# The meta tokens' values from one stationary tile: u's high and low columns side by side

## The chip, the cores and the metric

The kernel runs on 1 core of one Trainium2 chip. The metric is the device time of one execution in microseconds (us); a lower time is better. Times before are 2316.95, 2318.2 and 2320.6 us, median 2318.2 us.

## The reference

One layer of a hybrid decoder: a Mamba-2 branch (SSD) and a gated-linear-attention branch (GLA), gated and merged. 16 learned meta tokens stand ahead of the 2048 real tokens; they feed the states of both branches and are dropped from the output. Cut to what the change touches:

```python
u = rmsnorm(hres, norm_w)                       # (16 + 2048, 1024)
z, xbc, dt_raw, q, k, v, g_gla, a_lr, merge_g = split_cols(u @ w_in, IN_WIDTHS)
...
# GLA, 4 heads, dk = 128, dv = 256; S_t = diag(a_t) S_{t-1} + k_t^T v_t
o_m, st_m = gla_chunked(q[:, :m], k[:, :m], v[:, :m], log_a[:, :m], N_META, st0)   # m = 16
o_r, _ = gla_chunked(q[:, m:], k[:, m:], v[:, m:], log_a[:, m:], GLA_CHUNK, st_m)
```

The state after the meta tokens is, per head, the sum over the 16 tokens of (k times its decay to the end) outer v: a matrix of 128 x 256. All arithmetic is float32.

## The kernel before

The first stage runs over the real tokens in 4 blocks of 512; block 0 has the 16 meta tokens as well (`m0` = 16). Each block does 4 SSD groups (`ssd_proj`) and then 4 GLA heads (`gla_proj`); the recurrences (`ssd_scan`, `gla_scan`) are generators that advance a step whenever a projection yields, so that their work stands between the projections'. The second stage (gates, branch projections, output) follows.

Matmuls of float32 precision are made of float32r passes: every operand is split into a high part and a low part, and `accum` makes three passes, high x high, high x low and low x high (lines 189 to 191). So the page shows each product as three lines. In `proj_tok` (values and z) 128 tokens of u are the stationary operand, 128 of its rows (one of 8 `kt`) at a time, and the weights' columns move. `u` is one tile with the high and low part, `whl` a tile of weights with both parts: in block 0 it is made from raw weights by ScalarE (ACT, line 176, the high part) and GpSimd (POOL, line 177, the low part), kept in DRAM, and loaded from there in later blocks. `proj_tok` loads two `whl` tiles, runs over all chunks of tokens, yields, and does the same with the other two.

For the values of a head in block 0 there are five chunks of tokens: four of real tokens and one that begins at token 0, whose first 16 rows are the meta tokens. All 128 rows of it are computed (PSUM tile `pv5`, in the trace `pt`), and the first 16 are copied to SBUF (`vm`, line 658; in the trace `c`). In `gla_scan`, `kd` (line 715, a tile `act`) is k times its decay. Its 16 meta columns are transposed by TensorE (PE, line 770), copied to SBUF (`btm`, line 772, a tile `bt`), and multiplied with `vm` to give the state `s_gla` (lines 784 and 785). The tiles with the tag `bt` share two buffers in turn; the SSD scan uses them too.

The order on PE and on SyncE (SP, which issues most DMAs) is that of the code, by hand; on VectorE (DVE), ACT and POOL the framework's scheduler chooses it.

Of the kernel before, what the change touches and what calls it, by code (L numbers as in the profile page):

```python
# [7 lines left out]
F32 = mybir.dt.float32  # L8
F32R = mybir.dt.float32r
BF16 = mybir.dt.bfloat16  # L10
U8 = mybir.dt.uint8
AF = mybir.ActivationFunctionType
ALU = mybir.AluOpType

P = 128
D = 1024
KT = 8
META = 16
BLK = 512
NCH = BLK // P  # L20
SG = 4
# [7 lines left out]
NC1 = 6  # L29
# [11 lines left out]
def trunk_kernel(ctx: ExitStack, tc: tile.TileContext, xm, xmt, w_feat, w_tok, w_zm, w_br, w_o,  # L41
                 cf32, cmsk, pvec, fnw, hvec, gw2, out):
    nc = tc.nc
# [5 lines left out]
    def mk(pool, shape, dt, tag, **kw):  # L49
        cnt[0] += 1  # L50
        return pool.tile(shape, dt, tag=tag, name=f"{tag}_{cnt[0]}", **kw)
# [76 lines left out]
    wk = first.enter_context(tc.tile_pool(name="wk", bufs=2))  # L128
# [6 lines left out]
    def bank(pool, tag):  # L135
        return mk(pool, [P, 512], F32, tag)
# [3 lines left out]
    ident = cst[:, 0, :]  # L140
# [24 lines left out]
    def load_w(key, src):  # L165
        n = src.shape[-1]
        hl = mk(wpool, [P, 2, 512], F32R, "whl", bufs=4)[:, :, :n]
        if key in kept:
            nc.sync.dma_start(hl.bitcast(F32), kept[key])
        else:  # L170
            save(2)
            raw = mk(wpool, [P, 512], F32, "wr", bufs=NWR)[:, :n]
            nc.sync.dma_start(raw, src)
            if u_stores and len(kept) > 2:
                nc.sync.dma_start(*u_stores.pop(0))
            nc.scalar.activation(hl[:, 0], raw, AF.Copy)  # L176
            nc.gpsimd.tensor_tensor(hl[:, 1], raw, hl[:, 0].bitcast(F32), op=ALU.subtract)  # L177
            kept[key] = wdram.tile([P, 2, n], F32, tag="k_" + key, name="k_" + key, bufs=1)
            unsaved.append((kept[key], hl.bitcast(F32)))
        return hl[:, 0], hl[:, 1]  # L180
# [6 lines left out]
    def accum(ps, stat, mov, first, last, **kw):  # L187
        (sh, sl), (mh, ml) = stat, mov
        nc.tensor.matmul(ps, sh, mh, start=first, stop=False, **kw)  # L189
        nc.tensor.matmul(ps, sh, ml, start=False, stop=False, **kw)  # L190
        nc.tensor.matmul(ps, sl, mh, start=False, stop=last, **kw)  # L191
# [10 lines left out]
                    accum(ps[:, :n], (h[:, cs], lo[:, cs]), moving(kt, a, n), kt == 0, kt == KT - 1)  # L202
        return pss

    def proj_tok(key, src, u, starts, banks, width=256, per=2, sub=None):

        nq = KT // per
        opened = set()  # L210
        for q0 in range(0, nq, 2):
            if q0 == nq // 2:
                yield
            ws = [load_w(f"{key}_{q}", src[:, q * per * width:(q + 1) * per * width]) for q in (q0, q0 + 1)]
            for i, ((bk, ps), a) in enumerate(zip(banks, starts)):
                c0 = sub if sub is not None and i >= NCH else 0
                for k2 in range(2 * per):
                    kt = q0 * per + k2
                    h, lo = ws[k2 // per]
                    cs = slice(k2 % per * width + c0, (k2 % per + 1) * width)  # L220
                    accum(ps[:, c0:width], tuple(t[:, kt, a:a + P] for t in u),
                          (h[:, cs], lo[:, cs]), bk not in opened, kt == KT - 1, skip_group_check=True)
                    opened.add(bk)

    def halves_of(pool, tag):

        bks = [bank(pool, tag) for _ in range(2)]
        return bks, [(i // 2, bks[i // 2][:, i % 2 * 256:(i % 2 + 1) * 256]) for i in range(4)]

    def rstd_of(ssq, n, scale):  # L230
        r = mk(sm, [P, 4], F32, "rstd")
        nc.vector.tensor_scalar(r[:, :n], ssq, scale, EPS, op0=ALU.mult, op1=ALU.add)
        nc.gpsimd.tensor_tensor(r[:, :n], r[:, :n], mhalf[:, :n], op=ALU.pow)
        return r

    def split(h, lo, src):
        nc.scalar.activation(h, src, AF.Copy)
        nc.vector.tensor_tensor(lo, src, h.bitcast(F32), op=ALU.subtract)
# [134 lines left out]
    def new_block(b, u):  # L373
        o = Block()
        o.b, o.u = b, u
        o.m0 = META if b == 0 else 0
        o.tt = o.m0 + BLK
        o.segs_all = [(0, o.tt // 2), (o.tt // 2, o.tt // 2)] if b == 0 else [(0, BLK)]
        o.segs_real = [(o.m0, BLK)]
        o.starts = [o.m0 + c * P for c in range(NCH)]  # L380
        o.chunks = ([(0, META)] if o.m0 else []) + [(a, P) for a in o.starts]
        o.ci0 = 1 if o.m0 else 0
        o.nck = len(o.chunks)
        for nm in ("tkd", "tkc", "ntc", "wde", "ecu", "dec"):
            setattr(o, nm, mk(bpool, [P, 5, NH], F32, nm, bufs=1))
        o.cumd = mk(dpool, [NH, BLK], F32, "cumd")
        o.g_all = mk(bpool, [P, GH, META + BLK], F32, "g_all")
        o.alr = mk(bpool, [P, 5, 48], F32, "alr")
        o.mov = lambda kt, a, n: tuple(t[:, kt, a:a + n] for t in u)
        return o  # L390
# [88 lines left out]
    def ssd_proj(o, g):  # L479
# [3 lines left out]
        if g == 0:  # L483
            pss = [bank(*pl) for pl in [(pj, "pj")] * 3 + [(pt, "pt")] + ([(pc, "pc")] if m0 else [])]
            yield from proj_tok("zm", w_zm, o.u, o.starts + [0] * o.ci0, list(enumerate(pss)), 288, 1, 256)
            begin(dt_chain(o, pss[NCH:] + pss[:NCH]))
            done = [(ps[:, :256], zs[:, c]) for c, ps in enumerate(pss[:NCH])]
        else:
            pss, places = halves_of(pj, "pj")
            yield from proj_tok(f"z{g}", w_tok[g], o.u, o.starts, places)  # L490
            done = [(ps, zs[:, 2 * r:2 * r + 2].rearrange("p c f -> p (c f)")) for r, ps in enumerate(pss)]
# [154 lines left out]
    def gla_values(o, h):  # L646
        m0 = o.m0
        vh = mk(wk, [P, NCH, 256], F32R, "tok4", bufs=NT4)
        vl = mk(wk, [P, NCH, 256], F32R, "tok4", bufs=NT4)
        vm = None  # L650
        pss, places = halves_of(pj, "pj")
        if m0:
            vm = mk(wk, [P, 256], F32, "c1", bufs=NC1)[:META]
            pv5 = bank(pt, "pt")
            places.append((2, pv5[:, :256]))
        yield from proj_tok(f"v{h}", w_tok[SG + h], o.u, o.starts + [0] * o.ci0, places)
        if m0:
            nc.scalar.activation(vm, pv5[:META, :256], AF.Copy)
        for r, ps in enumerate(pss):
            split(*[t[:, 2 * r:2 * r + 2].rearrange("p c f -> p (c f)") for t in (vh, vl)], ps)  # L660
        return (vh, vl), vm
# [11 lines left out]
    def gla_proj(o, h):  # L673
        got = {"gs": []}
        keys = yield from gla_keys(o, h)
        last = o.b == nblk - 1
        if last and h == GH - 1:
            begin(gla_scan(o, h, *keys, got))
            yield
            got["v"] = yield from gla_values(o, h)  # L680
            yield
            yield from gla_gates(o, h - 1, held_gates.pop())
            yield from gla_gates(o, h, got["gs"])
        else:
            yield
            got["v"] = yield from gla_values(o, h)
            if last and h == GH - 2:
                begin(gla_scan(o, h, *keys, got))
                held_gates.append(got["gs"])
                yield  # L690
            else:
                yield
                yield from gla_gates(o, h, got["gs"])
                begin(gla_scan(o, h, *keys, got))
# [3 lines left out]
    def gla_scan(o, h, qs, kf, got):  # L698
# [7 lines left out]
        kd = mk(wk, [P, META + BLK], F32, "act", bufs=NACT)  # L706
# [5 lines left out]
        for c in range(NCH):  # L712
            cs = slice(m0 + c * P, m0 + (c + 1) * P)
# [53 lines left out]
        yield  # L767
        if m0:
            ps = bank(pt, "pt")
            nc.tensor.transpose(ps[:META, :P], kd[:, :META], ident)  # L770
            btm = mk(wk, [P, P], F32, "bt")
            nc.scalar.activation(btm[:META], ps[:META, :P], AF.Copy)
        ps = bank(pt, "pt")
        for c in range(NCH):
            nc.tensor.transpose(ps[:, c * P:(c + 1) * P], kd[:, m0 + c * P:m0 + (c + 1) * P], ident)
# [5 lines left out]
        yield  # L781
        if m0:
            ps = bank(pc, "pc")
            nc.tensor.matmul(ps[:, :256], btm[:META], got["v"][1], start=True, stop=True)
            nc.vector.tensor_copy(s_gla[:, h], ps[:, :256])
        level_out(32)
        level_in(8)
# [30 lines left out]
        for hl, n in parts:  # L818
            ps = bank(pt, "pt")
# [14 lines left out]
        ps = bank(pt, "pt")  # L834
# [20 lines left out]
        r = rstd_of(ssq, 4, 1.0 / 256)  # L855
# [4 lines left out]
        for j in range(2):  # L860
            ps = bank(pt, "pt")
# [25 lines left out]
    with tc.manual_schedule(engines={mybir.EngineType.PE, mybir.EngineType.SP}):  # L887
        for b in range(nblk):
            o = new_block(b, next_u[b])
# [221 lines left out]
    for si, st in enumerate(stages):  # L1111
        for q in range(28):
            p, j = PS[q // 4], q % 4
# [113 lines left out]
```

## Time and profile before

| | |
|---|---|
| median of 3 runs | 2318.2 us (2316.95 to 2320.6) |
| the profiled execution | 2309.24 us |
| its span, first to last instruction | 2307.5 us |
| mean granted TensorE clock | 0.993 |
| first stage, block 0 | up to about 480 us |
| first stage, the other blocks | to about 1510 us |
| second stage | from there to the end |

In the views, a line names the engine, the line of the kernel, the operation, the tile written and the tiles read. In a timeline the two numbers ahead of it are the start and the duration in us, x2 means merged neighbours, and a bracket at the end gives the idle time before it and what ended that. PE matmuls overlap: the time that one costs is the distance to the next start, not its duration. A shape like 128\*16 is rows x columns of the stationary operand; the one behind it is the moving operand's. PEld is the loading of the stationary operand. In a list of waits the numbers are total us, times and the longest.

### The profile page before, as it was taken

The page shows a single profiled execution, that of the slowest core. Times are in us where ns is not written, and L with a number is a line of the kernel's source. Part 1 is how long each engine was busy: PE and PEld are TensorE (multiplying, and loading weights), DVE is VectorE, ACT ScalarE, POOL GpSimd, SP SyncE. Part 2 cuts the span into 40 slices and gives each one's busy share as a digit, 9 for nine tenths or more (in the row PEclk, how much of TensorE's full clock was granted, in tenths as well). Part 3 has the DMA queues.
Part 4 walks back from the last instruction along what each step waited for, and adds up shares of the span by engine and source line. Part 5 has one row for each costly group of instructions (what it writes and reads, how often), then busy time and mean ns, then how long its engine had stood idle before and what let it go on. Part 6 is the DMA issues. An engine that isn't in the chain of part 4 may idle for free.

```text
span 2307.5 us, 36497 instructions
## 1 busy us (share of the span) xinstructions
PE 2229.4 (97%) x12651; PEld 1947.3 (84%) x12651; DVE 1623.4 (70%) x3144; ACT 1119.5 (49%) x2508; POOL 682.3 (30%) x677
## 2 busy tenths in 40 slices
PE   6899999999999999999999999989999999999998
PEld 6899988888889889888988898868788788787886
DVE  5787866687775677676578666664679854788876
ACT  5565654454444454444455334464554455454443
POOL 3344433122221122211122100136424264423341
PEclk9999999999999999999999999999999999999999
DMA  7766865667786676886667655466768866778653
GB/s 255 230 220 214 305 228 204 201 203 233 261 279 197 204 229 204 266 279 208 205 216 228 206 166 162 143 212 214 236 230 270 290 222 215 251 260 271 226 192 110
DMA packets 300937, 515.89 MB, mean 224 GB/s; under 512 B 27616, under 2 KB 143584, under 8 KB 300752
## 3 DMA queue, kind: packets, MB, share of 16 engines
q1 hardware_dynamic: 221840, 422.15, 56.1%
q10 hardware_dynamic: 78912, 91.41, 11.4%
q8 instruction: 99, 1.62, 0.3%
q14 instruction: 86, 0.70, 0.1%
HBM read 366.26 MB, written 147.19 MB: 223 GB/s over the span
## 4 chain that ended last, share of the span: by engine, by line
PE 68%; DVE 11%; DMA 9%; issue 5%; ACT 3%; POOL 2%; SPq 1%; ACTq 0%; DVEq 0%; POOLq 0%
PE pj L189 11%; PE pj L191 11%; PE pj L190 11%; PE psa L189 5%; PE psa L190 5%; PE psa L191 5%; PE psb L189 2%; PE psb L190 2%; PE psb L191 2%; PE pc L594 2%; DMA acc<-in_xmt 2%; PE pc L757 1%; DVE acc L508 1%; PE psc L189 1%; PE psc L190 1%
## 5 line engine op out<-in xcount | busy, mean ns | idle before, releaser
L189 PE MATMUL pj<-u,whl 128*128 128x512 f32 (+1 forms) x1184 | 445.5, 376 | 9.4 <-ACT acc L504 4.9
L191 PE MATMUL pj<-u,whl 128*128 128x512 f32 (+1 forms) x1184 | 430.1, 363 | 0.8 <-POOL whl L177 0.8
L190 PE MATMUL pj<-u,whl 128*128 128x512 f32 (+1 forms) x1184 | 429.3, 363 | 0.0
L189 PE MATMUL pj<-whl,u 128*128 128x256 f32 (+1 forms) x992 | 288.7, 291 | 3.2 <-ACT u L252 2.2
L191 PE MATMUL pj<-whl,u 128*128 128x256 f32 (+1 forms) x992 | 282.4, 285 | 0.2 <-DVE u L257 0.2
L190 PE MATMUL pj<-whl,u 128*128 128x256 f32 (+1 forms) x992 | 282.1, 284 | 0.4 <-POOL whl L177 0.4
L189 PE MATMUL psa<-b,a 128*128 128x512 f32 x640 | 252.4, 394 | 19.3 <-ACT sn L1001 15.8
L189 PEld LDWEIGHTS pj<-u,whl 128*128 128x128 f32 x1184 | 224.1, 189 | 47.9 <-ACT acc L504 5.7
L191 PEld LDWEIGHTS pj<-u,whl 128*128 128x128 f32 x1184 | 223.6, 189 | 36.6 <-POOL whl L177 1.1
L190 PEld LDWEIGHTS pj<-u,whl 128*128 128x128 f32 x1184 | 224.3, 189 | 33.2
L190 PE MATMUL psa<-b,a 128*128 128x512 f32 x640 | 251.3, 393 | 0.0
L191 PE MATMUL psa<-b,a 128*128 128x512 f32 x640 | 251.0, 392 | 0.0
L985 DVE TENSOR_TENSOR a<-ar,a 128x512 fp32r<-128x512 f32 x160 | 158.8, 1000 | 74.2 <-ACT a L984 73.9
L80 POOL TENSOR_TENSOR wr<-wr 128x256 f32<-128x256 f32 x80 | 68.4, 855 | 440.1 <-DMA wr<-u 179.8
L189 PEld LDWEIGHTS pj<-whl,u 128*128 128x128 f32 x992 | 189.6, 191 | 4.3 <-ACT u L252 2.4
L177 POOL TENSOR_TENSOR whl<-wr,whl 128x512 fp32r<-128x512 f32 (+1 forms) x100 | 136.5, 1372 | 190.7 <-ACT whl L176 151.4
L190 PEld LDWEIGHTS pj<-whl,u 128*128 128x128 f32 x992 | 189.8, 191 | 1.0 <-POOL whl L177 0.6
L191 PEld LDWEIGHTS pj<-whl,u 128*128 128x128 f32 x992 | 189.6, 191 | 0.8 <-DVE u L257 0.8
L961 DVE TENSOR_TENSOR b<-br,b 128x512 fp32r<-128x512 f32 x196 | 148.9, 781 | 40.2 <-ACT b L960 39.6
L975 POOL TENSOR_TENSOR as<-ar,ar 128x512 f32<-128x512 f32 x40 | 58.0, 1450 | 399.5 <-DMA ar<-in_w_br 134.2
L508 DVE SCALAR_TENSOR_TENSOR acc<-cin,hcw,acc 128x512 f32<-128x512 f32 (+1 forms) x192 | 159.4, 830 | 13.9 <-ACT acc L504 11.8
L960 ACT ACTIVATE b<-br 128x512 fp32r<-128x512 f32 x196 | 118.9, 626 | 94.3 <-DMA br<-br_t 33.0
(280 smaller groups left out, 5026.6 us busy)
## 6 DMA issues: line engine op xcount, KB each, us to landing
whl<-k_s SPq DMA_DIRECT2D x96, 512.0 KB, 4.4
whl<-k_g SPq DMA_DIRECT2D x96, 512.0 KB, 4.1
whl<-k_v SPq DMA_DIRECT2D x48, 512.0 KB, 4.1
whl<-k_z SPq DMA_DIRECT2D x36, 512.0 KB, 4.2
wr<-in_w_feat SPq DMA_DIRECT2D x64, 256.0 KB, 4.3
k_s<-whl SPq DMA_DIRECT2D x32, 512.0 KB, 3.7
cb<-cumd ACTq DMA_DIRECT2D x64, 256.0 KB, 5.8
y<-gg ACTq DMA_DIRECT2D x64, 256.0 KB, 4.7
```

The costliest lines, as they stand in the source:

```text
L80: nc.gpsimd.tensor_tensor(o, x, y, op=ALU.subtract)
L177: nc.gpsimd.tensor_tensor(hl[:, 1], raw, hl[:, 0].bitcast(F32), op=ALU.subtract)
L189: nc.tensor.matmul(ps, sh, mh, start=first, stop=False, **kw)
L190: nc.tensor.matmul(ps, sh, ml, start=False, stop=False, **kw)
L191: nc.tensor.matmul(ps, sl, mh, start=False, stop=last, **kw)
L508: nc.vector.scalar_tensor_tensor(acc, cin[:, k:k + tt], hcw[:, ti, k:k + 1], acc, op0=ALU.mult, op1=ALU.add)
L594: nc.tensor.matmul(py[:, h * 64:(h + 1) * 64], dm[:, h], xdt[:, h], start=True, stop=True)
L757: nc.tensor.matmul(ps[:, r * P:(r + 1) * P], kq[:, 2 * r * P:(2 * r + 1) * P], kq[:, (2 * r + 1) * P:(2 * r + 2) * P], start=True, stop=True)
L960: nc.scalar.activation(t[:, 0], raw, AF.Copy)
L961: nc.vector.tensor_tensor(t[:, 1], raw, t[:, 0].bitcast(F32), op=ALU.subtract)
L975: nc.gpsimd.tensor_tensor(s1, a21, a22, op=ALU.add)
L985: nc.vector.tensor_tensor(t[:, 1], src, t[:, 0].bitcast(F32), op=ALU.subtract)
```

## The change

The meta tokens get a stationary tile of their own, `both`: for each of the 8 `kt`, 16 columns of u's high part and 16 of its low part beside them. POOL copies them once, in block 0. Each `kt` takes two passes with it, one with the weights' high part moving and one with the low part, which give 32 rows: 16 from u's high part, 16 from its low part. All four products are in there (before, low x low was left out). The two halves are not added; instead the meta columns of kd are written twice side by side (`kdm`, by DVE), transposed as 32 columns, and the state's matmul sums over 32 rows. The output of the rest is unchanged.

```diff
-    def proj_tok(key, src, u, starts, banks, width=256, per=2, sub=None):
+    def proj_tok(key, src, u, starts, banks, width=256, per=2, sub=None, both=None):
...
+                    if both is not None and i >= NCH:
+                        for part in (h, lo):
+                            nc.tensor.matmul(ps[:2 * META], both[:, kt], part[:, cs], start=kt == 0 and part is h,
+                                             stop=kt == KT - 1 and part is lo)
+                        continue
                     accum(ps[:, c0:width], tuple(t[:, kt, a:a + P] for t in u),
...
+        o.both = None
+        if o.m0:
+            o.both = mk(wk, [P, KT, 2 * META], F32R, "both", bufs=1)
+            for i in range(2):
+                nc.gpsimd.tensor_copy(o.both[:, :, i * META:(i + 1) * META], u[i][:, :, :META].bitcast(F32))
...
-            vm = mk(wk, [P, 256], F32, "c1", bufs=NC1)[:META]
+            vm = mk(wk, [P, 256], F32, "c1", bufs=NC1)[:2 * META]
...
-            nc.scalar.activation(vm, pv5[:META, :256], AF.Copy)
+            nc.scalar.activation(vm, pv5[:2 * META, :256], AF.Copy)
...
-            nc.tensor.transpose(ps[:META, :P], kd[:, :META], ident)
+            kdm = mk(wk, [P, P], F32, "bt")[:, :2 * META]
+            nc.vector.tensor_copy(kdm.rearrange("p (r t) -> p r t", r=2),
+                                  kd[:, :META].unsqueeze(1).to_broadcast([P, 2, META]))
+            nc.tensor.transpose(ps[:2 * META, :P], kdm, ident)
...
-            nc.scalar.activation(btm[:META], ps[:META, :P], AF.Copy)
+            nc.scalar.activation(btm[:2 * META], ps[:2 * META, :P], AF.Copy)
...
-            nc.tensor.matmul(ps[:, :256], btm[:META], got["v"][1], start=True, stop=True)
+            nc.tensor.matmul(ps[:, :256], btm[:2 * META], got["v"][1], start=True, stop=True)
```

Behind the change the lines of the file stand a few numbers higher: 606 is 616, 715 is 725, 720 is 730, 770 is 783, 775 is 788.

On PE, at the second burst of head 0's values, before (names with their buffer numbers; pj is a bank of real tokens, pt the bank of the meta tokens):

```order
L191 MATMUL pj_3062<-whl_3177,u_255 128x256
L189 MATMUL pt_3064<-whl_3170,u_255 128x256
L190 MATMUL pt_3064<-whl_3170,u_255 128x256
L191 MATMUL pt_3064<-whl_3170,u_255 128x256
...
L189 MATMUL pt_3064<-whl_3177,u_255 128x256
L190 MATMUL pt_3064<-whl_3177,u_255 128x256
L191 MATMUL pt_3064<-whl_3177,u_255 128x256
L570 MATMUL pt_3251<-cst,act_2498 128x128
```

The three passes stand twice for each of the two `whl` tiles, 12 in all. The same place of the change:

```order
L191 MATMUL pj_3065<-whl_3176,u_255 128x256
L223 MATMUL pt_3067<-whl_3169,both_372 32x256 x4
L223 MATMUL pt_3067<-whl_3176,both_372 32x256 x4
L580 MATMUL pt_3246<-cst,act_2501 128x128
L580 MATMUL pt_3246<-cst,act_2598 128x128
```

8 passes with 32 rows of output stand there now; what is ahead and behind is the same.

On DVE, at head 0's kd (act_3529), before; L606 and L607 belong to the SSD scan of the last group, L248 to the next block's u:

```order
L605 TENSOR_TENSOR c_525_3516<-c_525_3516,pc_3506 128x256
L715 TENSOR_TENSOR act_3529<-act_3529,act_2936 128x528
L720 TENSOR_TENSOR act_3541<-act_3541,act_2861 128x512
L606 TENSOR_TENSOR c_525_3516<-c_525_3516,tok_432_3025 128x256
L607 TENSOR_TENSOR tok_432_3025<-c_525_3516,tok_301_2227 128x256
L248 SCALAR_TENSOR_TENSOR acc_3874<-acc_3874,pv,cin_3380 128x512
```

The same place of the change, where kd is act_3524:

```order
L615 TENSOR_TENSOR c_526_3511<-c_526_3511,pc_3501 128x256
L725 TENSOR_TENSOR act_3524<-act_3524,act_2939 128x528
L730 TENSOR_TENSOR act_3536<-act_3536,act_2864 128x512
L616 TENSOR_TENSOR c_526_3511<-c_526_3511,tok_433_3028 128x256
L781 COPY bt_3629<-act_3524 128x32
L617 TENSOR_TENSOR tok_433_3028<-c_526_3511,tok_302_2230 128x256
L253 SCALAR_TENSOR_TENSOR acc_3863<-acc_3863,pv,cin_3375 128x512
```

The new copy stands two instructions behind the one that makes kd. For heads 1 and 2 it stands behind that head's L730, for head 3 behind an update of `s_gla` that follows L725.

On POOL, at the first weights (whl_468 to whl_522 are those of z and dt), in the change:

```order
L177 TENSOR_TENSOR whl_468<-wr_470,whl_468 128x288
L177 TENSOR_TENSOR whl_476<-wr_478,whl_476 128x288
L397 CAST both_372<-u_255 128x8x16 x2
L177 TENSOR_TENSOR whl_514<-wr_516,whl_514 128x288
L177 TENSOR_TENSOR whl_522<-wr_524,whl_522 128x288
```

Before, the four splits follow each other without the casts. SP's order is the same in both. On DVE and ACT a few more neighbours change places in block 0; behind block 0 every engine's order is the same.

More of the change, by code (lines that the diff above doesn't have):

```diff
@@ L652, in gla_values @@
         if m0:
-            vm = mk(wk, [P, 256], F32, "c1", bufs=NC1)[:META]
+            vm = mk(wk, [P, 256], F32, "c1", bufs=NC1)[:2 * META]
             pv5 = bank(pt, "pt")
             places.append((2, pv5[:, :256]))
-        yield from proj_tok(f"v{h}", w_tok[SG + h], o.u, o.starts + [0] * o.ci0, places)
+        yield from proj_tok(f"v{h}", w_tok[SG + h], o.u, o.starts + [0] * o.ci0, places, both=o.both)
         if m0:
-            nc.scalar.activation(vm, pv5[:META, :256], AF.Copy)
+            nc.scalar.activation(vm, pv5[:2 * META, :256], AF.Copy)
         for r, ps in enumerate(pss):
```

## The prediction

> **What bounds the kernel now.** I read the page first, then the waits of the stretch that the change touches, then the timelines of single places.
>
> ```profile
> span 2307.5 us, 36497 instructions
> PE 2229.4 (97%) x12651; PEld 1947.3 (84%) x12651; DVE 1623.4 (70%) x3144; ACT 1119.5 (49%) x2508; POOL 682.3 (30%) x677
> PE 68%; DVE 11%; DMA 9%; issue 5%; ACT 3%; POOL 2%; SPq 1%; ACTq 0%; DVEq 0%; POOLq 0%
> ```
>
> TensorE (PE) is busy for 97% of the span, and the chain that ended last runs over it for 68%. A pass that PE no longer runs is therefore worth its time, unless PE then waits longer for something that isn't driven by PE itself. The list of PE's waits in 230 to 480 us, where block 0 handles the four GLA heads, has just this:
>
> ```profile
> PE pc L847 <- DVE s_gla L848: 2.8, 2, 2.3
> PE pc L757 <- DVE s_gla L785: 0.9, 1, 0.9
> PE pj L190 <- POOL whl L177: 0.4, 1, 0.4
> ```
>
> Three lines, 4.1 us in 250: PE leads here, and VectorE (DVE) holds it up at three places, the longest of them 2.3 us.
>
> **The passes that go.** The groups of lines by form in 0 to 480 us, and one burst of the timeline (its first two and last starts, and what follows it):
>
> ```profile
> L191 PE MATMUL pt<-whl,u 128*128 128x256 f32 x32 | 9.0, 282 | 0.0
> L189 PE MATMUL pt<-whl,u 128*128 128x256 f32 x32 | 9.0, 281 | 0.0
> L190 PE MATMUL pt<-whl,u 128*128 128x256 f32 x32 | 9.0, 281 | 0.0
> ...
> 239.26 0.28 PE L189 MATMUL pt<-whl,u 128*128 128x256 f32 x1
> 239.38 0.28 PE L190 MATMUL pt<-whl,u 128*128 128x256 f32 x1
> ...
> 240.56 0.28 PE L191 MATMUL pt<-whl,u 128*128 128x256 f32 x1
> 240.68 1.04 PE L629 MATMUL pt<-cst,tok 128*128 128x128 f32 x8
> ```
>
> The meta tokens' values take 3 x 32 = 96 passes: 4 heads, each with two bursts of 12. The 281 ns are a pass from start to end; passes overlap, and what one costs is the distance of starts: 240.68 - 239.26 = 1.42 us for 12, 0.118 us each, 11.4 us in all. Afterwards there are 64 passes with 256 columns of weights moving and a stationary tile of 32 columns. The trace has no such pass. Its nearest rows are these: 512 moving columns on a stationary of 128, and 32 moving columns on a stationary of 128.
>
> ```profile
> 255.06 0.40 PE L189 MATMUL pj<-u,whl 128*128 128x512 f32 x1
> 255.29 0.39 PE L190 MATMUL pj<-u,whl 128*128 128x512 f32 x1
> ...
> 28.47 0.26 PE L191 MATMUL pc<-whl,u 128*128 128x32 f32 x1
> 28.58 0.26 PE L189 MATMUL pc<-whl,u 128*128 128x32 f32 x1
> ```
>
> Starts are 0.23 us apart with 512 columns, so 256 columns would want 0.115 by what they move. With 32 moving columns they are still 0.11 apart, which the moving can't explain: that is the loading of 128 stationary columns. At 256 both limits stand close together, so a narrow stationary gains little per pass. Bounds: 0.109 (a little below the 0.11 of the load) and 0.118 (as now). I take 0.115, which is the half of the 512 row. Then 64 x 0.115 = 7.4 us, and PE saves 11.4 - 7.4 = 4.0 us: 1.0 per head, 0.5 per burst; with the bounds, 3.8 to 4.4.
>
> A rule on the load can be weighed here.
>
> ```profile
> L770 PEld LDWEIGHTS pt<-cst,act x4: 87/90/90, 280.8 to 427.8; 128*16 128x16 f32 x4
> L775 PEld LDWEIGHTS pt<-cst,act x64: 138/141/146, 280.9 to 1450.6; 128*128 128x128 f32 x64
> ```
>
> A load of 16 columns takes 90 ns here, one of 128 takes 141. The Trainium skill, page "TensorE: Matmul & The Clock Gate", section "LDWEIGHTS (loading the stationary operand)", says that the load costs its number of columns over 1.2 ns, so a quarter here, and its gap for 256 moving columns is 109 ns; by it the saving would be 11.4 - 64 x 0.109 = 4.4 us. The trace agrees in direction and by less than that proportion.
>
> **What is added on PE's path.** Per head, DVE now writes the meta columns of kd twice side by side (L781 of the changed file), before PE may transpose them. The price of that copy is bounded by an operation on twice its elements and one on a thirty-second:
>
> ```profile
> 430.51 0.22 DVE L417 TENSOR_TENSOR dx<-tkd,nega 128x64 f32<-128x64 f32 x1
> 432.05 0.16 DVE L232 TENSOR_SCALAR rstd<-ssq 128x4 f32<-128x4 f32 x1
> ```
>
> I take 0.2 us. As DVE work that is nothing (4 x 0.2 in 480 us at 70%). But its place counts: the transpose stands ahead of the four kd transposes and of level_out(64) in PE's order. For head 0 the trace of before shows:
>
> ```profile
> 278.26 0.69 DVE L715 TENSOR_TENSOR act<-act,act 128x528 f32<-128x528 f32 x1
> 278.88 1.78 DVE L720 TENSOR_TENSOR act<-act,act 128x512 f32<-128x512 f32 x1
> 280.57 1.50 DVE L606 TENSOR_TENSOR c<-c,tok 128x256 f32<-128x256 f32 x1
> 282.11 0.43 DVE L607 TENSOR_TENSOR tok<-c,tok 128x256 f32<-128x256 f32 x1
> ...
> 280.80 0.28 PE L191 MATMUL pj<-u,whl 128*128 128x264 f32 x1
> 280.92 0.27 PE L770 MATMUL pt<-cst,act 128*16 128x128 f32 x1
> 281.03 0.60 PE L775 MATMUL pt<-cst,act 128*128 128x128 f32 x4
> ```
>
> L715 ends kd at 278.95, 1.97 us ahead of PE's transpose at 280.92: no wait today. The scheduler has put the copy behind L606, which ends at 282.07; so the copied tile is there at 282.3. PE, 1.0 us earlier by head 0's two bursts, both ahead of it, comes at 279.9. If DVE stays where it is, PE waits 2.4 us and leaves 1.4 later than before; if DVE moves forward with PE by the whole 1.0, PE waits 1.4 and leaves 0.4 later. I take the middle: +0.9 us against before. What is queued behind the waiting transpose is PE's alone: ScalarE (ACT) takes the transposed tiles at 284.83 and 286.59, so nobody else is held.
>
> ```profile
> 284.83 0.25 ACT L772 ACTIVATE bt<-pt 16x128 f32<-16x128 f32 x1
> 286.59 0.57 ACT L237 ACTIVATE kdt<-pt 128x512 fp32r<-128x512 f32 x1
> ```
>
> For heads 1 to 3 the copy stands behind L720 or L715 and ahead of a DVE instruction that waits for PE, in an idle stretch of DVE:
>
> ```profile
> 329.76 0.48 DVE L848 SCALAR_TENSOR_TENSOR s_gla<-s_gla,egl,pc 128x256 f32<-128x256 f32 x1 [5.82 <-PE pc L847]
> 377.93 0.48 DVE L848 SCALAR_TENSOR_TENSOR s_gla<-s_gla,egl,pc 128x256 f32<-128x256 f32 x1 [3.73 <-PE pc L847]
> ```
>
> The idle 5.82 and 3.73 us cover 0.2 us (head 3's copy stands right behind the L848 after that one, and its transpose comes at 427.8 only). Nothing there.
>
> **Where the saving goes on the way.** The next wait of PE is the 2.29 us at 322.09:
>
> ```profile
> 297.44 0.28 PE L189 MATMUL pt<-whl,u 128*128 128x256 f32 x1
> ...
> 306.69 0.98 DVE L248 SCALAR_TENSOR_TENSOR acc<-acc,pv,cin 128x512 f32<-128x512 f32 x1 [1.01 <-DMA acc<-in_xmt]
> ...
> 322.09 0.70 PE L847 MATMUL pc<-s_gla,act 128*128 128x256 f32 x2 [2.29 <-DVE s_gla L848]
> ...
> 346.48 0.28 PE L189 MATMUL pt<-whl,u 128*128 128x256 f32 x1
> ...
> 355.87 0.45 DVE L764 COPY_PREDICATED c<-msk,pc 128x256 f32<-128x256 uint8 x1 [2.08 <-PE pc L757]
> ```
>
> Up to there PE has +0.9 from head 0's wait and -1.0 from head 1's bursts (the second at 297.44): about zero. DVE's run ahead of that wait begins with a landing DMA (306.69), not with PE, so even a gain would mostly be waited away there. I book heads 0 and 1 together as 0. DVE's next long run (355.87) begins with a PE result, after both bursts of head 2 (the second at 346.48), so it moves forward with PE, and head 2's 1.0 stays; likewise head 3's, behind that run. From 480 us on all engines' orders are unchanged.
>
> **The rest.** POOL gets two casts of 128 elements per partition each, between the sixth and the seventh split of the first weights:
>
> ```profile
> 29.34 2.38 POOL L177 TENSOR_TENSOR whl<-wr,whl 128x288 fp32r<-128x288 f32 x2 [9.79 <-ACT whl L176]
> 33.16 0.81 POOL L177 TENSOR_TENSOR whl<-wr,whl 128x288 fp32r<-128x288 f32 x1 [1.44 <-ACT whl L176]
> ...
> 30.17 2.12 DVE L257 TENSOR_TENSOR u<-act,u 128x528 fp32r<-128x528 f32 x2 [0.35 <-ACT u L252]
> ```
>
> The second cast needs u's last low part, at 30.17 + 2.12 = 32.29. The split of 288 elements takes 0.81, the cast less; it ends by 33.1, and the split behind it waits for ACT until 33.16 anyway. Cost 0, and if that cover were gone, at most the 0.81. SyncE's queue is unchanged. On ACT a few splits of weights stand one or two places elsewhere; PE waited for POOL's half of such a split for 0.4 us in this whole stretch, so I price it at nothing, with half a us either way. The wider eviction (32 for 16 partitions) and the state's matmul over 32 rows have the same free sizes as before: 0.
>
> **Sum.** -4.0 (passes) + 0.9 (head 0's wait) + 1.1 (taken up by the wait at 322 us) = -2.0 us. The profiled execution took 2309.2 us (span 2307.5); it becomes 2307.2. The runs' median is 2318.2, 9 us above the profiled one, so I apply the difference there: 2316.2 us.
>
> **Rivals.** First, the whole saving arrives: head 0's copy isn't felt or DVE's runs all move forward with PE. For it speaks that PE leads nearly everywhere; against it L606 at 280.57. It gives -4.0, with the lower price per pass -4.4: 2314.2.
>
> Second, on the other side: going from a stationary of 128 columns to one of 32 and back costs PE its overlap. The price is a pass's whole length less the distance of starts, 0.28 - 0.12 = 0.16 us each way, 8 bursts x 2 x 0.16 = 2.6 us; against -2.0 that is +0.6: 2318.8. It decides from 2.0 / 16 = 0.125 us per change on. Against it speaks the row of L770 above: a stationary of 16 columns between two of 128, 0.12 us after its predecessor and 0.11 ahead of its successor, no loss either way. The Trainium skill, page "TensorEngine Tiling (Array Packing)", section "Key Properties", says that changing the tiling mode drains the engine; by that rule this rival would hold, and the trace's L770 doesn't show it.
>
> Third, the four heads' savings all vanish in DVE's waits (2.3 and 0.9 us, and the 2.8 - 2.3 = 0.5 us of the second wait for s_gla): no change, 2318.2. Against it: DVE's run of head 2 begins with PE.
>
> **Numbers.** Forecast 0.55 (its own range -0.5 to -3.5 us), whole saving 0.25, lost overlap 0.12, nothing 0.08. All of them lie within the 0.2% (4.6 us) that about can be told from no change, so "same" holds most: faster by more needs the whole saving and a run to the good side (0.13), slower by more a lost overlap twice as dear (0.06). The range goes from the whole saving at its best, 2313.8, less the 2.4 us by which single runs stand off their median, to the lost overlap, 2318.8, plus 2.4: 2311.5 to 2321.2.
>
> **What would show it.** 64 passes out of "both", their starts 0.109 to 0.118 us apart, bursts of 0.9 to 0.95 us for 1.42; a PE wait of 1.4 to 2.4 us for DVE's copy at about 280 us and none for the other three; the wait for s_gla at about 320 us still at 2 us or more; PE about 2 us ahead of before at 480 us and from there on. Wrong I would be if starts lie 0.2 us apart at the bursts' edges, if the copy waits for its buffer, or if PE's lead at 480 us is gone at 1500.

## The result and the profile after

The changed kernel takes 2311.95 us (median; 2304.12 to 2320.08), the kernel before beside it 2317.05 us (2310.84 to 2324.73). The ratio is 0.9977, its 95% interval 0.9968 to 0.9985. Timed twice more against the kernel before on other chips it gave 0.9985 (0.9975 to 0.9996) and 0.9972 (0.9958 to 0.9987). The three weighted together are about 0.9979 (0.9973 to 0.9985), 4.9 us less, with 3.5 to 6.3 as the interval. So it is a little faster, by an amount at the edge of the 0.2% named in the prediction, and by more than the 2.0 us that were forecast.

The profiled executions do not say so by their ends. The page of the changed kernel:

```profile
span 2312.7 us, 36442 instructions
PE 2232.9 (97%) x12619; PEld 1948.0 (84%) x12619; DVE 1619.9 (70%) x3148; ACT 1120.2 (48%) x2508; POOL 680.3 (29%) x679
PE 64%; DMA 14%; DVE 11%; issue 5%; ACT 3%; SPq 1%; POOL 1%; ACTq 0%; DVEq 0%; POOLq 0%
```

This execution's span is 5.2 us above the one shown before the change, with 32 matmuls fewer. One execution is no measure of 5 us here: four traces of the kernel before ended at 2307.5, 2309.8, 2311.1 and 2319.2 us. What a trace can show is the place of the change, since each burst and each wait stands there by itself. PE's waits in 225 to 480 us after the change (total us, times, longest):

```profile
PE pt L783 <- DVE bt L781: 2.6, 1, 2.6
PE pj L190 <- POOL whl L177: 1.0, 1, 1.0
PE pc L860 <- DVE s_gla L861: 0.8, 2, 0.5
PE pc L767 <- DVE s_gla L798: 0.7, 1, 0.7
```

The first line is new: PE waits for DVE's copy, once, for 2.6 us. The wait for `s_gla` at 322 us (L847 before, L860 now), 2.3 us at its longest, has nearly gone.

**The passes.** PE's timeline at the first burst of head 0, and the groups of the new passes and of their weight loads (duration least/median/most in ns, then first and last start):

```profile
238.99 0.28 PE L191 MATMUL pj<-whl,u 128*128 128x256 f32 x1
239.11 1.08 PE L223 MATMUL pt<-whl,both 128*32 128x256 f32 x8
240.02 0.27 PE L639 MATMUL pt<-cst,tok 128*128 128x128 f32 x1
...
L223 PEld LDWEIGHTS pt<-whl,both x64: 107/108/108, 239.0 to 394.5; 128*32 128x32 f32 x64
```

The burst takes 240.02 - 239.11 = 0.91 us where 12 passes took 1.42: 0.114 us a pass, against the 0.115 forecast. Eight bursts save 8 x 0.51 = 4.0 us of PE's work, as the sum had it. The step into the narrow stationary is 239.11 - 238.99 = 0.12 us, and eight passes fit into 0.91 with the step out: nothing is lost at the edges, so the second rival falls. The Trainium skill, page "TensorEngine Tiling (Array Packing)", section "Key Properties", has the engine drain at a change of tiling mode. The trace shows no such loss between 128 and 32 stationary columns on 128 rows; whether that is a change of mode in the page's sense, no run here shows.

**The copy of head 0.** DVE's timeline, and what PE did with it:

```profile
280.88 1.48 DVE L616 TENSOR_TENSOR c<-c,tok 128x256 f32<-128x256 f32 x1
282.28 0.17 DVE L781 COPY bt<-act 128x32 f32<-128x32 f32 x1
...
282.50 0.40 PE L783 MATMUL pt<-cst,bt 128*32 128x128 f32 x1 [2.58 <-DVE bt L781]
```

The copied tile was forecast for 282.3 and a wait of up to 2.4 us; it came at 282.45, behind L616 (the copy is the third instruction behind the one that makes kd), and the wait was 2.58. PE leaves at 282.50, 1.6 us later than the 280.92 of before: both are a little over the bounds of the prediction (2.4 and 1.4).

**Behind it.** The prediction says nothing of what follows. Engine busy times in a window of this trace; the number behind POOL's is the granted TensorE clock (PEclk):

```profile
282.10:285.50 3.40, 3.00 (x15) 3.00 (x16) 2.85 (x9) 2.50 (x8) 1.22 (x2) 0.50 0.99 325
```

The clock was 0.50 for 3.4 us. PE's first transpose of kd (L788, L775 before) starts 1.7 us later than before, 282.69 for 281.03, and behind the slow stretch it is 3.0 us late (a pass of L190 starts at 290.00 for 287.00): the halved clock cost 1.3 us. Head 1's bursts gave 1.0 back, and about 0.5 went at small places. So PE was 2.44 us late when it reached the wait at 322 us (322.24 for 319.80, a start less the wait ahead of it). It hardly had to wait there any more:

```profile
322.54 0.70 PE L860 MATMUL pc<-s_gla,act 128*128 128x256 f32 x2 [0.30 <-DVE s_gla L861]
```

It starts 0.45 us later than the 322.09 before. The other side of this wait is DVE's run up to that `s_gla`. Its first and last instruction in the change, and its last one before (its first one before is the L248 at 306.69, shown in the prediction):

```profile
308.55 0.75 DVE L253 SCALAR_TENSOR_TENSOR acc<-acc,pv,cin 128x512 f32<-128x512 f32 x1 [0.43 <-DMA acc<-in_xmt]
322.01 0.47 DVE L861 SCALAR_TENSOR_TENSOR s_gla<-s_gla,egl,pc 128x256 f32<-128x256 f32 x1
...
321.56 0.47 DVE L848 SCALAR_TENSOR_TENSOR s_gla<-s_gla,egl,pc 128x256 f32<-128x256 f32 x1
```

From start to start the run took 14.87 us before and takes 13.46 now, with one long operation fewer (two of 1.3 to 1.4 us, before three of 1.4 to 1.8), and it begins 1.86 us later where PE is 2.44 later. So of the 2.0 us that this wait lost, 1.4 come from a shorter run and 0.6 from a run that begins nearer to PE. That PE was late for its slow clock is not the reason, as `copyonly`, `heads01` and `heads123` will show. Why the run is shorter wasn't tried.

### The profile page after: what moved, and what is told of

It is laid out like the page before. It is cut to its first block, busy times and chain, and to the rows that moved or that the text cites. A ratio compares the mean times of both kernels' runs of the same rounds, so it can differ in the third digit from the quotient of the medians.

```text
span 2312.7 us, 36442 instructions
## 1 busy us (share of the span) xinstructions
PE 2232.9 (97%) x12619; PEld 1948.0 (84%) x12619; DVE 1619.9 (70%) x3148; ACT 1120.2 (48%) x2508; POOL 680.3 (29%) x679
## 4 chain that ended last, share of the span: by engine, by line
PE 64%; DMA 14%; DVE 11%; issue 5%; ACT 3%; SPq 1%; POOL 1%; ACTq 0%; DVEq 0%; POOLq 0%
PE pj L189 11%; PE pj L191 10%; PE pj L190 10%; PE psa L189 4%; PE psa L190 4%; PE psa L191 4%; PE psb L191 2%; PE psb L189 2%; PE psb L190 2%; DMA acc<-in_xmt 2%; DMA br<-br_t 2%; PE pc L767 2%; PE pc L604 1%; DVE acc L518 1%; DMA cb<-cumd 1%
## 5 line engine op out<-in xcount | busy, mean ns | idle before, releaser
L190 PE MATMUL pj<-u,whl 128*128 128x512 f32 (+1 forms) x1184 | 429.6, 363 | 0.0
L190 PE MATMUL pj<-whl,u 128*128 128x256 f32 (+1 forms) x992 | 282.2, 285 | 1.0 <-POOL whl L177 1.0
L191 PE MATMUL pj<-whl,u 128*128 128x256 f32 (+1 forms) x992 | 282.3, 285 | 0.2 <-DVE u L262 0.2
L190 PE MATMUL psa<-b,a 128*128 128x512 f32 x640 | 253.4, 396 | 0.0
L190 PEld LDWEIGHTS pj<-u,whl 128*128 128x128 f32 x1184 | 224.2, 189 | 33.1
L998 DVE TENSOR_TENSOR a<-ar,a 128x512 fp32r<-128x512 f32 x160 | 150.0, 943 | 79.9 <-ACT a L997 77.3
L177 POOL TENSOR_TENSOR whl<-wr,whl 128x512 fp32r<-128x512 f32 (+1 forms) x100 | 136.3, 1370 | 192.2 <-ACT whl L176 159.4
L190 PEld LDWEIGHTS pj<-whl,u 128*128 128x128 f32 x992 | 190.0, 191 | 1.6 <-POOL whl L177 1.2
L189 PEld LDWEIGHTS psa<-b,a 128*128 128x128 f32 x640 | 122.8, 192 | 51.3 <-ACT sn L1014 21.9
```

What stands on the lines that cost most here:

```text
L998: nc.vector.tensor_tensor(t[:, 1], src, t[:, 0].bitcast(F32), op=ALU.subtract)
```

## The experiments

In the texts on record, theory A is the forecast's working, and the other letters are rivals to it. Times of the kernel before on the same chip are 2315.62 us for the first four kernels, 2314.44 for the next four, 2317.38 for the last four.

### The two kernels again (before_again, after_again)

> The kernel before, once more, for a second profile and for what a ratio of equal kernels looks like: 1.000 within 0.1%. In its trace the 12 passes of a burst take 1.42 us, TensorE waits about 2.3 us for s_gla at 322 us and not for kd at 281 us. Single profiles differ by some us in the second stage with where the halved clock falls.

> The changed kernel, once more. Theory A (block 0 gives 2 to 3 us, the rest of the measured 5 us is spread of the runs and the clock): ratio 0.9985 to 0.9990, and at 480 us TensorE is 2 to 2.5 us ahead of before, at 1500 us about the same. Theory B (the change also moves something in the second stage): ratio 0.9975 to 0.998 again, and against the new profile of before the lead grows by 2 us or more behind 1510 us where the granted clock is equal.

Before against itself gave 0.9999 (0.9985 to 1.0014); the change 0.9985 (0.9975 to 0.9996), the edge of theory A's range. PE was 2.1 us ahead of the first trace of before at 480 us and 0.4 at 1500, and the growing lead of theory B isn't there. In this trace of the change the copy fell differently:

```profile
279.22 1.28 DVE L781 COPY bt<-act 128x32 f32<-128x32 f32 x1
280.55 0.28 PE L783 MATMUL pt<-cst,bt 128*32 128x128 f32 x1 [0.57 <-DVE bt L781]
291.75 0.71 PE L767 MATMUL pc<-sq 128*128 128x128 f32 x4 [1.29 <-DVE s_gla L798]
322.14 0.70 PE L860 MATMUL pc<-s_gla,act 128*128 128x256 f32 x2 [0.32 <-DVE s_gla L861]
```

The long operation on DVE was now the copy itself (1.28 us for 0.17), L616 the short one. PE waited 2.0 us less at the copy, 1.29 us at the next state update, had its clock halved behind that (from 292.7 us on), and started 0.4 us earlier at 322 us than in the first trace. The size of the wait at the copy isn't what decides; what follows takes up most of the difference.

### The copy without its reason, and the copy made early (copyonly, early)

`copyonly` keeps before's three passes and has only the doubled copy and the transpose of 32 columns:

```diff
-            nc.tensor.transpose(ps[:META, :P], kd[:, :META], ident)
+            kdm = mk(wk, [P, P], F32, "bt")[:, :2 * META]
+            nc.vector.tensor_copy(kdm.rearrange("p (r t) -> p r t", r=2), ...)
+            nc.tensor.transpose(ps[:2 * META, :P], kdm, ident)
...
```

> The kernel before with its three passes, and of the change only the doubled kd with its copy on VectorE and its transpose of 32 columns. Theory A: TensorE waits about 1.4 us at 281 us, the wait at 322 us shrinks by as much to about 0.9 us, and from 330 us on TensorE stands where it stood before: ratio 1.000. Rival (the wait is a real loss): 1.4 us or more behind before at 480 us, and with a halved clock after the wait 2 to 3 us (0.1%).

It gave 1.0008 (0.9996 to 1.002). Its waits:

```profile
PE pt L773 <- DVE bt L771: 2.6, 1, 2.6
PE pc L850 <- DVE s_gla L851: 2.3, 2, 1.8
```

PE waits at the copy as in the change, and, other than there, still 1.8 us at 322 us. Its clock also was 0.50 behind the copy, from 283.8 us on, and at 491 us PE was 2.7 us later than in the first trace of before. That is the rival's number (2 to 3 us), not theory A's: in this trace the copy isn't absorbed. The time can't tell it from no change. PE came to the wait at 322 us 3.2 us later than before (323.02 for 319.80) and still waited 1.76: being late for the copy and the slow clock took only 0.5 us off it. DVE's run ahead of it took 15.4 us here.

`early` makes the doubled columns by a small multiply of their own, ahead of the one that makes the other columns of kd, and has the rest of the change:

```diff
-        nc.vector.tensor_tensor(kd[:, :tt], kd[:, :tt], kf[:, :tt], op=ALU.mult)
+        if m0:
+            kdm = mk(wk, [P, P], F32, "bt")[:, :2 * META]
+            nc.vector.tensor_tensor(kdm..., kd[:, :META]..., kf[:, :META]..., op=ALU.mult)
+        nc.vector.tensor_tensor(kd[:, m0:tt], kd[:, m0:tt], kf[:, m0:tt], op=ALU.mult)
...
```

> The change, but the doubled meta columns of kd come from a multiplication of their own ahead of kd's, so that VectorE makes them before the long multiplications of head 0. Theory A (what heads 0 and 1 save is taken up by the wait for s_gla at 322 us): the wait of 2.6 us at 282 us goes, the wait at 322 us is back at 2.3 us or more, and the lead of TensorE at 480 us stays 2 to 2.5 us; time as the change within 0.5 us. Rival (the wait at 282 us is a real loss): lead of about 4 us at 480 us, time 1.5 to 2 us (0.08%) below the change.

It gave 0.9995 (0.9985 to 1.0005), no better than the change. The wait at 282 us is gone, and two others have grown:

```profile
PE pc L772 <- DVE s_gla L800: 3.3, 2, 2.2
PE pc L862 <- DVE s_gla L863: 2.6, 2, 2.2
...
289.49 0.75 DVE L253 SCALAR_TENSOR_TENSOR acc<-acc,pv,cin 128x512 f32<-128x512 f32 x1 [2.20 <-DMA acc<-in_xmt]
291.54 0.42 DVE L800 COPY s_gla<-pc 128x256 f32<-128x256 f32 x1
...
292.01 0.71 PE L772 MATMUL pc<-sq 128*128 128x128 f32 x4 [2.25 <-DVE s_gla L800]
```

The next limit stands 10 us behind the copy: DVE waits for a landing DMA with L253, and the `s_gla` that PE needs is queued behind. What PE gains at 282 us it waits away at 292. The second of the two 2.2 us is a like wait at 371 us, 0.5 in the change. Behind both the clock was 0.50 for 3.4 us. Neither theory has this: the wait at 322 us stayed at 0.4 us, and at 480 us PE was 1.8 us behind the first trace of before.

### The change in two halves (heads01, heads23)

```diff
-        yield from proj_tok(f"v{h}", w_tok[SG + h], o.u, o.starts + [0] * o.ci0, places, both=o.both)
+        yield from proj_tok(f"v{h}", w_tok[SG + h], o.u, o.starts + [0] * o.ci0, places,
+                            both=o.both if h in (0, 1) else None)
...
```

and the same condition at `kdm`, `btm` and the state's matmul; `heads23` has `(2, 3)`.

> The change for heads 0 and 1 alone; heads 2 and 3 as before. Theory A (VectorE sets the pace from 280 to 322 us, so what these two heads save is waited away there): TensorE waits 0.6 to 2.6 us in all for the copy and for s_gla around 280 to 292 us, the wait at 322 us falls from 2.3 to about 0.3 us, and from 322 us on TensorE stands within 0.5 us of where it stood before, but for halved clocks; ratio 0.9992 to 1.0002. Rival (every saved pass counts): 2 us ahead from 322 us on, ratio 0.9991 like heads 2 and 3 alone.

> The change for heads 2 and 3 alone; heads 0 and 1 as before. Theory A: the wait of 2.3 us at 322 us stays as before, no wait at 282 us, and TensorE gains 0.5 us at each of four bursts behind it, 2.0 us at 400 us and still 2 us at 480 us; of the change's gain at 480 us (2.0 to 2.3 us) this is all. Ratio 0.999, the change's own less what a halved clock behind the wait at 322 us costs. Rival: about half of the change's gain, 1 us at 480 us.

Heads 0 and 1 alone gave 0.9989 (0.9978 to 1.0000), heads 2 and 3 alone 0.998 (0.9966 to 0.9994). Both have the right sign, with intervals of 5 us and more; the first lies just outside theory A's range. The traces part them better. At the wait at 322 us:

```profile
320.57 0.70 PE L865 MATMUL pc<-s_gla,act 128*128 128x256 f32 x2 [0.32 <-DVE s_gla L866]
```

```profile
322.59 0.70 PE L865 MATMUL pc<-s_gla,act 128*128 128x256 f32 x2 [2.26 <-DVE s_gla L866]
```

The first row is that of heads01, the second that of heads23. With heads 0 and 1 the wait is short, though no halved clock made PE late: DVE's run ahead of it took 13.5 us in heads01 and 14.9 in heads23. PE starts 1.5 us earlier than in the first trace of before in heads01, where theory A allowed 0.5.

### The passes by themselves (wide, double)

`wide` also has two passes per `kt`, but on 128 stationary columns, those of u's high part (`both` is made and not used; u's low part is left out of the meta tokens' values). `double` makes each of the change's passes twice, 128 in all (the meta tokens' values count double).

```diff
-                            nc.tensor.matmul(ps[:2 * META], both[:, kt], part[:, cs], ...)
+                            nc.tensor.matmul(ps, u[0][:, kt, a:a + P], part[:, cs], ...)
```

```diff
-                        for part in (h, lo):
+                        for r, part in enumerate((h, lo, h, lo)):
...
```

> Two passes per kt as in the change, but with 128 columns of u's high part as the stationary tile in place of the 32 columns of both; u's low part is left out of the meta tokens' values. My theory (the moving columns set the pace, the loading of 128 columns costs nearly as much): starts 0.118 us apart for 0.114 us with 32 columns, a burst of 8 takes 0.95 us for 0.91, time as the change plus 0.2 us. Rival (the narrow stationary is the gain): starts clearly over 0.12 us. Rival (narrow stationary drains the engine): the edges of the change's bursts are dearer than those here.

> The change with its two passes run twice into the same sums (so the meta tokens' values count double), 64 passes more, 7.3 us of TensorE. Theory A: heads 0 and 1 hide part of their 3.7 us in VectorE's waits (the wait at 282 us shrinks, the one at 322 us is small already), heads 2 and 3 count in full: 4 to 6 us over the change at 480 us, ratio 1.0000 to 1.0010 against before. Rival (all hidden): as the change. Rival (all counts): 7.3 us over the change, ratio 1.0012.

`wide` gave 0.9981 (0.9966 to 0.9995), `double` 1.0025 (1.001 to 1.0039). A burst of `wide` and the start behind it, then one of `double`:

```profile
239.54 1.11 PE L223 MATMUL pt<-whl,u 128*128 128x256 f32 x8
240.49 0.27 PE L639 MATMUL pt<-cst,tok 128*128 128x128 f32 x1
```

```profile
241.67 1.98 PE L223 MATMUL pt<-whl,both 128*32 128x256 f32 x16
243.49 0.93 PE L639 MATMUL pt<-cst,tok 128*128 128x128 f32 x7
```

0.95 us for 8 passes on 128 columns, 0.119 each as before; 0.91 on 32 columns; 1.82 for 16, 0.114 each. Of the 0.51 us that a burst saves, 0.47 come from four passes fewer and 0.04 from the narrow stationary. From 64 to 128 passes the time rises by 0.40 to 0.53% (the change's three ratios), 9 to 12 us, with 4 to 5 us of uncertainty and partly on different chips; PE's own work rises by 64 x 0.114 = 7.3. That misses theory A (1.0000 to 1.0010); the rival by which all of it counts (1.0012) is within the interval. So more passes cost time, but whether each counts in full the times can't say.

### The long wait and the clock (before_3, before_4, after_3, heads123)

Here theory B stands for the whole saving of 4 us, and theory C was added: the wait at 322 us is dearer than its length, since the clock is at times halved behind it.

> The kernel before, once more, for its trace. Theory A (the saving of heads 0 and 1 is taken up by DVE's run alone): PE's wait for s_gla at 322 us is 2 to 2.5 us again, and PE's position at 348 us agrees with the first trace of before within 0.5 us. Theory C (the long wait is dearer than its length, since the granted clock is sometimes halved for 3.41 us behind it, which costs 1.7 us more): the wait is the same, but the position at 348 us is either that of the first trace (no halved clock there) or 1.5 to 2 us later (halved).

> The kernel before, for its trace, as the run ahead of it; theories as there. If neither run of the two has a halved clock between 322 and 328 us, theory C has it in 1 of 4 traces of before, and its mean price is 0.4 us, too little for the missing 2 us.

> The change, once more. The forecast's size (theory A): ratio 0.9991 (2.0 us). The whole saving (theory B): 0.9983 (4.0 us). With the intervals so far pooled at 0.9980, B is the likelier: I expect 0.9977 to 0.9987. In the trace: the wait at 322 us below 0.7 us, no halved clock behind it, PE 0.5 to 2.5 us ahead of the first trace of before at 480 us.

`heads123` is the change without head 0 (`h in (1, 2, 3)`), so without the copy that PE waits for.

> The change for heads 1, 2 and 3 only; head 0 keeps its three passes and has no copy. Theory A: no wait at 282 us; head 1's 1.0 us comes off as a longer wait at 322 us (2.3 to 3.3 us), heads 2 and 3 give 2.0: ratio 0.9991. Theory B (whole saving): 3.0 us, 0.9987. Theory C: as A, but the long wait at 322 us stays, and with it now and then the halved clock behind it: less gain than with all four heads, by 1 us or more.

The wait in the two traces of before, and the clock behind the first of them:

```profile
321.40 0.86 PE L847 MATMUL pc<-s_gla,act 128*128 128x256 f32 x2 [2.29 <-DVE s_gla L848]
...
321.80:325.20 3.40, 3.40 (x17) 3.31 (x16) 2.63 (x3) 2.63 (x10) 1.28 (x1) 0.50 0.18 70
```

```profile
320.19 0.70 PE L847 MATMUL pc<-s_gla,act 128*128 128x256 f32 x2 [1.37 <-DVE s_gla L848]
```

At 348 us PE stood 0.9 us later (before_3) and 1.9 us earlier (before_4) than in the first trace: neither theory's number, since the way up to the wait differs from trace to trace too. So the way behind it is better read by itself. PE runs the same instructions there in each kernel, but for the passes of heads 2 and 3. The table has PE's start behind the wait at 322 us, the way from there to a matmul in `pc` (L190, at 330.03 us in the first trace of before), the way from that to one in `pj` (L190, at 480.08), and the start of the output transposes of head 3 (L863 of before). All times are in us:

| trace | passes of heads 2, 3 | clock halved behind 322 | start at 322 | 322 to 330 | 330 to 480 | start at 491 |
|---|---|---|---|---|---|---|
| before | three | no | 322.09 | 7.94 | 150.04 | 490.66 |
| before_4 | three | no | 320.19 | 7.94 | 150.01 | 488.21 |
| heads01 | three | no | 320.57 | 7.94 | 150.02 | 488.92 |
| before_again | three | yes | 322.37 | 9.49 | 150.01 | 491.94 |
| before_3 | three | yes | 321.40 | 9.50 | 150.02 | 490.99 |
| heads23 | two | yes | 322.59 | 9.51 | 148.06 | 490.76 |
| after | two | no | 322.54 | 7.94 | 147.78 | 488.32 |
| after_again | two | no | 322.14 | 7.94 | 147.94 | 488.62 |
| after_3 | two | no | 322.83 | 7.94 | 147.74 | 489.11 |
| heads123 | two | no | 322.26 | 7.94 | 147.96 | 488.76 |

From 330 to 480 us the five traces with three passes agree within 0.03 us, and two passes take 1.9 to 2.3 us less: 2.2 on the mean of the change's three, which the sum had as 2.0. From 322 to 330 us a halved clock costs 1.56 us, and nothing else changes that stretch. It came in two of four traces of before and in none of the change's. The change's clock was halved earlier, between 281 and 296 us, in all three of its traces. That isn't what shortens the wait at 322 us: heads01 and heads123 have no halved clock between 150 and 490 us, and wait 0.32 and 0.30 us there.

At 491 us the three traces of the change have a mean of 488.7, the four of before 490.45: 1.8 us, beside the 2.0 forecast. That fits, but the four of before lie 3.7 us apart there, so these means alone prove little; the 2.2 us of heads 2 and 3 don't hang on that spread.

In `after_3` the wait was 0.77 us (below 0.7 was expected), no halving came behind it, and PE was 1.6 us ahead of the first trace at 491 us. The times say more. It gave 0.9972 (0.9958 to 0.9987), a little below the 0.9977 to 0.9987 expected, and `heads123` gave 0.9952 (0.9933 to 0.9971), outside the expectation of every theory, though at 491 us it stands where the change does. It is the fastest kernel measured, but rests on 5 timed executions (2306.35 to 2310.72 us) for the others' 11 or more, and it wasn't timed again. What makes it faster behind 491 us stays open.

## Why the prediction was right, and where it wasn't

- **The bound.** PE was named as the bound, and the direction holds: less time with 64 passes, more with 128.
- **The passes, -4.0 us.** Right: 1.42 to 0.91 us a burst, 0.114 a pass. The 0.109 of the lower bound was a little too good. So was the gap of the Trainium skill, page "TensorE: Matmul & The Clock Gate"; it stands there in the section "Back-to-back issue gap", not in the one that the prediction names. The load's rule, of the Trainium skill, page "TensorE: Matmul & The Clock Gate", section "LDWEIGHTS (loading the stationary operand)", would make a load of 32 columns an estimated 27 ns; the record is 108. The price was near the moving side's (half of the 512 row), so this didn't matter. That the 0.11 us at 32 moving columns are the loading of 128 stationary ones, as the prediction has it, no run shows.
- **Head 0's copy, +0.9 us.** The place and the cause were right, the bounds too narrow on both sides. PE waited 2.58, 0.57 and 2.77 us in the three traces of the change, where 1.4 to 2.4 were forecast. In the first it left 1.6 us later than before (bound 1.4), in after_again 0.4 us earlier (bound 0.4 later), since DVE's long operations fell elsewhere.
- **The wait at 322 us, +1.1 us.** Heads 0 and 1 together were booked as 0, and that is right within what the traces tell: PE starts 0.45 us later than before in the first pair and 1.0 later on the mean of three against four traces (322.5 for 321.5), and the halved clock behind before's wait, 2 of 4 x 1.56 = 0.8 us of its mean, takes most of that back. But it came right by luck, since the way was another. PE was to wait 2 us or more there as before, and waited 0.3 to 0.8. The halved clock behind the copy, 1.3 us in the first trace, was missing in the sum, and so was the one behind before's wait. And the premise failed that DVE's run, as it begins with a landing DMA, doesn't move with PE: in the four traces of before it begins at 305.74 to 306.98 us, each time 0.6 to 0.7 us behind the same instruction of PE (the first L821 on `sq`). In the change it begins nearer to PE, and in two of three traces it is 1.4 us shorter.
- **Heads 2 and 3, -2.0 us.** Right: -2.2 in a stretch that repeats within 0.03 us.
- **POOL and the rest, 0.** Right at the place that was argued: the casts end at 32.46 us, less than the 33.1 allowed, and PE waits for nothing there.

```profile
32.17 0.29 POOL L397 CAST both<-u 128x128 fp32r<-128x128 f32 x1 [0.63 <-DVE u L262]
```

- **The total, -2.0 us.** Too small: -4.9 (3.5 to 6.3) by the times, where the own range of the forecast went to -3.5, and the first rival (-4.0 or -4.4) has the better number, though not for its reason, since the copy is felt. As far as is known, the step that failed is the last one: that the difference at 480 us is the difference at the end. 1.8 us are shown at 491 us; the other 3 were not located, and their cause stays open. They are not the mean clock: over the 52 timed executions of before and 23 of the change in the two later comparisons it is 0.990 for both, with 2316.4 and 2312.2 us on average. They can't be read from single traces either, whose way from 491 us to the end is 1817 to 1831 us in before and 1823 to 1825 in the change. The prediction's sign of being wrong, a lead that is gone at 1500 us, can't be decided by them: against the first trace of before the change's three are 2.6 and 0.4 us ahead and 3.3 behind there, the other three of before 0.3 and 1.0 ahead and 4.4 behind.
- **The range.** 2311.95 lies in it, but only by the 2.4 us that were put on for the spread of single runs: the whole saving at its best was 2313.8. That is luck rather than foresight.

## What to carry to other kernels

A matmul pass costs the distance of starts, and a burst's price is its count of passes times that; a narrow stationary alone gives little where 256 columns move. Before a small operation is put on another engine ahead of a waiting PE, see what stands ahead of it in that engine's order and what PE will wait for next: taking the wait away (early) only moved it 10 us on. Where single executions differ by more than the effect, compare traces over the shortest way that holds the change, and leave the total to many timed executions.

## What was not expected of the hardware

- Behind some waits of PE of 1.3 to 2.8 us the granted clock is 0.50 for 3.4 us (windows above), and starts of 256-column passes go from 0.12 to 0.21 us apart. Behind the wait at 322 us it came in two of three traces of before in which that wait was 2.2 to 2.3 us long. The clock's records in the 14 traces show a part of what decides. In each trace the starts of all halved stretches lie whole multiples of 3.413 us apart, within 0.01 us, so the clock goes by windows that don't heed the kernel. Between 225 and 1490 us all 22 windows in which PE was idle for 1.9 us or more were followed by a halved one. Of the others there, with 1.83 us or less, two were: one with 1.29 us (after_again), and one that was itself halved (double). In this stretch, then, a wait halves the clock when enough of it falls into one window. Outside it windows with as little as 0.8 us were also followed by a halved one, and some of up to 2.24 us in the first 150 us were not, so idle time isn't the whole rule.

  Before's wait of 2.29 us was cut by a border at 321.37 us, that of before_3 was not. PE's busy time is the first number behind the length, the granted clock the one behind POOL's; the window that follows in before_3 is shown above, at 0.50:

```profile
317.95:321.36 3.41, 1.86 (x15) 1.60 (x13) 3.24 (x7) 1.72 (x6) 1.05 (x1) 1.00 0.79 274
321.37:324.78 3.41, 2.69 (x20) 2.64 (x21) 2.37 (x5) 3.41 (x12) 1.45 (x1) 1.00 0.32 77
...
318.40:321.80 3.40, 1.11 (x10) 0.88 (x8) 3.02 (x9) 2.85 (x9) 0.00 (x0) 1.00 0.77 245
```

  The Trainium skill, page "TensorE: Matmul & The Clock Gate", section "What's actually happening", has a free-running window of 3413 ns, with which this agrees; its "after ≥1 idle window (~3.4µs)" does not agree with halving behind windows that were idle for 1.9 to 2.8 us.
- DVE's copy of 32 columns took 0.17 us in one place and 1.28 in another of the same kernel:

```profile
L781 DVE COPY bt<-act x4: 168/464/1277, 282.3 to 379.0; 128x32 f32<-128x32 f32 x4
```

  In both traces POOL makes two splits of weights just then (L177, from 278.97 to 282.08 us in the first, 278.34 to 281.96 in the second), and two DVE operations are long in each: L730 (1.77 us) and L616 (1.48) in the first, the copy (1.28) and L253 (1.76) in the second, where L616 took 0.42. Which of them it hits changes from one execution to the next. Each of the four ends 0.04 to 0.6 us behind the end of one of those splits. That fits POOL as the cause, but it was not tried.
